# A streaming gradient: stores and loads on two queues in timed pairs, instead of one queue in triples

## The chip, the cores and the metric

The kernel runs on one core of a Trainium2 chip. A core has a vector engine (DVE), a scalar engine (ACT), GpSimd (POOL), a matrix engine that is not used here, and a sequencer for transfers (SP). SP, ACT and POOL can each issue DMAs; the bytes are moved by 16 DMA engines, from HBM to the on-chip memory SBUF (128 partitions) or back. The metric is device microseconds (us) for one execution; lower is better.

## What is computed

`reference(x)` is `np.gradient(x, axis=1)` for `x` of 8192 x 8192 float32. In each row, an inner element is half the difference of its right and left neighbours; the first element is `x[1] - x[0]`, the last `x[m-1] - x[m-2]`. Each element is read once and written once: 268.44 MB in, 268.44 MB out.

## The kernel before, in words

The 8192 rows are cut into 32 sets of 256 (`nsets`). A set puts two consecutive rows (`R = 2`) on each of 128 partitions, so that a partition holds 16,384 elements, 64 KiB, and one DMA moves 8.39 MB. There are three buffers, `slot0` to `slot2` (`NB = 3`); set i uses slot i mod 3. A slot is 64 elements (`SH`) wider than a set: the load writes at offset 64, the result is written from offset 0 in the same slot, so that the vector engine's pass writes behind where it reads.

For each set i, in the loop at lines 66 to 93:

- POOL (line 70) takes the four end differences of each partition's two rows into `ends`, as soon as the load has landed.
- DVE (line 76) makes one pass over 16,382 elements, a custom operation that subtracts two shifted views and halves, in place. It also writes wrong values at the row ends.
- The ends are copied over them (line 87), four elements per partition: by DVE for 20 sets, by POOL for 12.
- SP issues the store (line 89).
- After every third set SP issues the next three loads (lines 91 to 93, through `load`, line 60). Each of them waits until the store that last used the slot has landed.

Every DMA is issued by SP and goes into one queue, q1, in this order: loads 0, 1, 2, stores 0, 1, 2, loads 3, 4, 5, stores 3, 4, 5, and so on, to stores 30 and 31. The order within each engine is written out by hand (`manual_schedule`); `chain` (lines 45 to 56) tells the framework which steps an instruction must really wait for, and takes out the other dependences within a slot.

Of the kernel before, what the change touches and what calls it, by code (L numbers as in the profile page):

```python
# [1 line left out]

# [4 lines left out]


@with_exitstack
def kernel(  # L10
    ctx: ExitStack,
    tc: tile.TileContext,
    x: bass.AP,
    out: bass.AP,
):

    nc = tc.nc
    P = nc.NUM_PARTITIONS
    n, m = x.shape
    R = 2
    NB = 3  # L30
    SH = 64
    W = R * m
    nsets = n // (P * R)
    f32 = x.dtype

    x_sets = x.rearrange("(s p t) m -> s p (t m)", p=P, t=R)
    out_sets = out.rearrange("(s p t) m -> s p (t m)", p=P, t=R)

    pool = ctx.enter_context(tc.tile_pool(name="pool", bufs=1))
    slots = [pool.tile([P, SH + W], f32, name=f"slot{k}", tag=f"slot{k}") for k in range(NB)]  # L40
    ends = pool.tile([P, nsets, R, 2], f32, name="ends", tag="ends")
    loads, stores = [], [None] * nsets
    in_front = {}

    def chain(i, ins, *needed):

        group, engine = f"slot{i % NB}", ins.ins.engine
        keep = [o.ins for o in needed]  # L50
        if in_front.get(engine, (None,))[0] == group:
            keep.append(in_front[engine][1])
        tc.declare_no_dep(ins.ins, group=group, keep=keep, reason="implied by the needed step")
        tc.add_to_no_dep_group(group, ins.ins)
        in_front[engine] = group, ins.ins
        return ins

    def load(i):
        b = slots[i % NB]
        ins = nc.sync.dma_start(out=b[:, SH : SH + W], in_=x_sets[i])  # L60
        loads.append(chain(i, ins, *([stores[i - NB]] if i >= NB else [])))

    with tc.manual_schedule():
        for i in range(NB):
            load(i)
        for i in range(nsets):
            b = slots[i % NB]
            xin = b[:, SH : SH + W].rearrange("p (t m) -> p t m", m=m)

            ins = nc.gpsimd.tensor_sub(  # L70
                out=ends[:, i, :, :],
                in0=xin[:, :, 1 : m : m - 2],
                in1=xin[:, :, 0 : m - 1 : m - 2],
            )
            at = [chain(i, ins, loads[i])]
            ins = nc.vector._custom_dve(  # L76
                dve_ops.TENSOR_TENSOR_REDUCE_SUB_MAX,
                out=b[:, 1 : W - 1],
                in0=b[:, SH + 2 : SH + W],
                in1=b[:, SH : SH + W - 2],  # L80
                s0=0.0,
                s1=0.5,
            )
            halved = chain(i, ins, *at)
            res = b[:, 0:W].rearrange("p (t m) -> p t m", m=m)
            placer = nc.gpsimd if i % 5 in (1, 3) and i < nsets - 2 else nc.vector
            ins = placer.tensor_copy(out=res[:, :, 0 : m : m - 1], in_=ends[:, i, :, :])  # L87
            placed = chain(i, ins, halved)
            ins = nc.sync.dma_start(out=out_sets[i], in_=b[:, 0:W])
            stores[i] = chain(i, ins, placed)  # L90
            if i % NB == NB - 1:
                for k in range(i + 1, min(i + 1 + NB, nsets)):
                    load(k)


# [1 line left out]
_INS = ['x']  # L97
_OUTS = [((8192, 8192), 'float32')]


# [23 lines left out]
```

## Time and profile before

| what | value |
|---|---|
| time, median of 3 runs | 1247.73 us (1247.55 to 1247.99) |
| the profiled execution: span from first to last instruction | 1245.7 us |
| moved | 536.88 MB, 431 GB/s over the span |
| DVE pass over a set (line 76) | 32 of 17.224 us |
| DMA issue by SP | 0.34 us each at the median |
| DMA issue to landing, median | 58.0 us loads, 40.4 us stores (with the time in the queue) |

The profiled execution is one run of the program under the hardware profiler, with its own time; times inside it are compared with its span, not with the median of the runs. "Span" goes from the first instruction to the last. "Busy" is the time in which an engine executes instructions; issuing a DMA is not counted. The DMA row gives, in 40 equal slices of the span, the busy share of the 16 DMA engines in tenths (9 is 90% or more). A group's row reads: line, engine, operation, output<-input with shapes, count, then busy time, mean nanoseconds of one, and the idle time ahead of it with what ended it. A row of waits reads: who waited, for whom, us in total, times, longest. In the timeline a row is start, duration, engine, line, operation.

### The profile page before, as it was taken

The page shows a single profiled execution, that of the slowest core. Times are in us where ns is not written, and L with a number is a line of the kernel's source. Part 1 is how long each engine was busy: PE and PEld are TensorE (multiplying, and loading weights), DVE is VectorE, ACT ScalarE, POOL GpSimd, SP SyncE. Part 2 cuts the span into 40 slices and gives each one's busy share as a digit, 9 for nine tenths or more (in the row PEclk, how much of TensorE's full clock was granted, in tenths as well). Part 3 has the DMA queues.
Part 4 walks back from the last instruction along what each step waited for, and adds up shares of the span by engine and source line. Part 5 has one row for each costly group of instructions (what it writes and reads, how often), then busy time and mean ns, then how long its engine had stood idle before and what let it go on. Part 6 is the DMA issues. An engine that isn't in the chain of part 4 may idle for free.

```text
span 1245.7 us, 237 instructions
## 1 busy us (share of the span) xinstructions
DVE 554.6 (45%) x52; POOL 8.8 (1%) x48
## 2 busy tenths in 40 slices
DVE  2850583069009702850582079009603840591083
POOL 0000000000000000000000000000000000000000
DMA  9999999999999999999999999999999999999999
GB/s 404 438 436 423 427 431 438 438 438 436 436 427 431 425 438 436 425 434 436 429 434 436 434 436 434 436 434 438 419 436 436 434 438 438 431 434 429 429 410 404
DMA packets 9217, 536.88 MB, mean 431 GB/s; under 512 B 1024, under 2 KB 1024, under 8 KB 1024
## 3 DMA queue, kind: packets, MB, share of 16 engines
q1 hardware_dynamic: 9216, 536.88, 99.8%
q14 instruction: 1, 0.01, 0.0%
HBM read 268.44 MB, written 268.44 MB: 431 GB/s over the span
## 4 chain that ended last, share of the span: by engine, by line
another core or an unknown queue 74%; DVE 18%; DMA 3%; issue 2%; POOL 1%; SPq 0%; POOLq 0%
DVE slot L76 18%; DMA slot<-in_x_dram 3%; POOL ends L70 0%; POOL slot L87 0%; SPq L60 0%; POOLq L119 0%; DVE slot L87 0%
## 5 line engine op out<-in xcount | busy, mean ns | idle before, releaser
L76 DVE CUSTOM_DVE_ANT_0 slot<-slot 128x16382 f32<-128x16382 f32 x32 | 551.2, 17224 | 668.7 <-POOL ends L70 668.7
L70 POOL TENSOR_TENSOR ends<-slot 128x4 f32<-128x4 f32 x32 | 6.3, 198 | 989.6 <-DMA slot<-in_x_dram 989.6
L87 POOL COPY slot<-ends 128x4 f32<-128x4 f32 x12 | 2.3, 190 | 207.9 <-DVE slot L76 207.9
L87 DVE COPY slot<-ends 128x4 f32<-128x4 f32 x20 | 3.4, 172 | 0.7
L108 POOL MEMSET const-bfloat16-1.0<- 128x1 bf16 x1 | 0.1, 101 | 0.0
L108 POOL MEMSET const-uint8-127<- 128x1 uint8 x1 | 0.1, 101 | 0.0
L108 POOL MEMSET const-float32-0.0<- 128x1 f32 x1 | 0.1, 98 | 0.2 <-issue 0.2
L108 POOL MEMSET const-float32-1.0<- 128x1 f32 x1 | 0.1, 98 | 0.0
## 6 DMA issues: line engine op xcount, KB each, us to landing
slot<-in_x_dram SPq DMA_DIRECT2D x32, 58.0
out_dram<-slot SPq DMA_DIRECT2D x32, 40.4
```

What stands on the lines that cost most here:

```text
L70: ins = nc.gpsimd.tensor_sub(out=ends[:, i, :, :], in0=xin[:, :, 1 : m : m - 2], in1=xin[:, :, 0 : m - 1 : m - 2],)
L76: ins = nc.vector._custom_dve(dve_ops.TENSOR_TENSOR_REDUCE_SUB_MAX, out=b[:, 1 : W - 1], in0=b[:, SH + 2 : SH + W], in1=b[:, SH : SH + W - 2],
L87: ins = placer.tensor_copy(out=res[:, :, 0 : m : m - 1], in_=ends[:, i, :, :])
L108: nc = _bacc.Bacc("TRN2", target_bir_lowering=False, num_devices=1)
```

## The change

Loads stay on SP, stores go to ACT, which has its own queue. Two loads are issued at the start instead of three. From then on a store of set i and the load of set i + 2 (`ahead`) go as a pair:

- For sets 1 to 30, DVE first makes a pass over a tile of zeros (`still`), 2500 elements wide (`FIRST`), into the front part of the slot of set i + 2. It waits until store i - 1, the last user of that slot, has landed.
- Then DVE copies the ends of set i (for all sets; POOL copies none), and ACT issues store i.
- For sets 0 to 29, DVE makes a second pass over zeros, 1700 elements wide (`THEN`), into the same slot behind the first; SP issues load i + 2 when this pass is done.

The load overwrites what the two passes wrote, so the passes change nothing in the result. DVE's order for a set is: the pass over the set, the 2500-wide pass, the copy of the ends, the 1700-wide pass. POOL fills the zeros once at the start (128 x 2502).

```diff
-            placer = nc.gpsimd if i % 5 in (1, 3) and i < nsets - 2 else nc.vector
-            ins = placer.tensor_copy(out=res[:, :, 0 : m : m - 1], in_=ends[:, i, :, :])
+            ahead = i + NB - 1
+            if 0 < i < nsets - 1:
+                pause(ahead, SH, FIRST, stores[i - 1])
+            ins = nc.vector.tensor_copy(out=res[:, :, 0 : m : m - 1], in_=ends[:, i, :, :])
             placed = chain(i, ins, halved)
-            ins = nc.sync.dma_start(out=out_sets[i], in_=b[:, 0:W])
+            ins = nc.scalar.dma_start(out=out_sets[i], in_=b[:, 0:W])
             stores[i] = chain(i, ins, placed)
-            if i % NB == NB - 1:
-                for k in range(i + 1, min(i + 1 + NB, nsets)):
-                    load(k)
+            if ahead < nsets:
+                load(ahead, pause(ahead, SH + FIRST, THEN))
```

The start has `for i in range(NB - 1): load(i)`. New are

```python
    FIRST, THEN = 2500, 1700
    still = pool.tile([P, 2 + FIRST], f32, name="still", tag="still")
    nc.gpsimd.memset(still, 0.0)
    def pause(i, at, width, *needed):
        ins = difference(slots[i % NB][:, at : at + width], still, width)
        return chain(i, ins, *needed)
```

where `difference(out, x, width)` is the custom operation of line 76 with its shifted views, used for the set's own pass too. `load(i, *needed)` now waits for what it is given instead of the store of set i - 3.

More of the change, by code (lines that the diff above doesn't have):

```diff
@@ L56, in chain, with load, difference @@
         return ins
-    def load(i):
+    def load(i, *needed):
         b = slots[i % NB]
         ins = nc.sync.dma_start(out=b[:, SH : SH + W], in_=x_sets[i])
-        loads.append(chain(i, ins, *([stores[i - NB]] if i >= NB else [])))
+        loads.append(chain(i, ins, *needed))
+    def difference(out, x, width):
+        return nc.vector._custom_dve(
+            dve_ops.TENSOR_TENSOR_REDUCE_SUB_MAX,
+            out=out,
+            in0=x[:, 2 : 2 + width],
+            in1=x[:, 0:width],
+            s0=0.0,
+            s1=0.5,
+        )
+    def pause(i, at, width, *needed):
+        ins = difference(slots[i % NB][:, at : at + width], still, width)
+        return chain(i, ins, *needed)
     with tc.manual_schedule():
-        for i in range(NB):
+        for i in range(NB - 1):
             load(i)
@@ L75 @@
             at = [chain(i, ins, loads[i])]
[L76 to L83, printed above, removed]
+            ins = difference(b[:, 1 : W - 1], b[:, SH : SH + W], W - 2)
             halved = chain(i, ins, *at)
             res = b[:, 0:W].rearrange("p (t m) -> p t m", m=m)
-            placer = nc.gpsimd if i % 5 in (1, 3) and i < nsets - 2 else nc.vector
-            ins = placer.tensor_copy(out=res[:, :, 0 : m : m - 1], in_=ends[:, i, :, :])
+            ahead = i + NB - 1
+            if 0 < i < nsets - 1:
+                pause(ahead, SH, FIRST, stores[i - 1])
+            ins = nc.vector.tensor_copy(out=res[:, :, 0 : m : m - 1], in_=ends[:, i, :, :])
             placed = chain(i, ins, halved)
-            ins = nc.sync.dma_start(out=out_sets[i], in_=b[:, 0:W])
+            ins = nc.scalar.dma_start(out=out_sets[i], in_=b[:, 0:W])
             stores[i] = chain(i, ins, placed)
-            if i % NB == NB - 1:
-                for k in range(i + 1, min(i + 1 + NB, nsets)):
-                    load(k)
+            if ahead < nsets:
+                load(ahead, pause(ahead, SH + FIRST, THEN))
 _INS = ['x']
```

## The prediction

> **What bounds the kernel now.** I read the page's head with its DMA lines first, then the waits of SP's queue, the groups of instructions, the timeline of the end, and last the trace's packet records one by one (the rows behind the DMA lines). The page:
>
> ```profile
> span 1245.7 us, 237 instructions
> ...
> DVE 554.6 (45%) x52; POOL 8.8 (1%) x48
> ...
> DMA  9999999999999999999999999999999999999999
> ...
> q1 hardware_dynamic: 9216, 536.88, 99.8%
> ```
>
> One queue, q1, keeps the 16 DMA engines busy for 99.8% of the span; DVE has work for 45%. The end is set by how fast an engine passes its bytes and by holes between its packets. The packet records: 8192 packets of 65,536 bytes, 512 for each engine (8 for each load or store), and 1024 of 4 bytes, one behind every eighth. The big one takes 2.418 us at the median (5th percentile 2.418, 95th 2.422), which is 27.1 GB/s, and the next starts as one ends: a DMA takes an engine 8 x 2.418 = 19.34 us, a load and a store 38.69.
>
> So the span is: first packet at 1.75, its extra latency 0.62 (3.04 against 2.42), 512 x 2.418 = 1238.0, then 4.1 of other losses, and 1.18 from the last packet's end (1244.49) to the end (1245.67). Of the 4.1 some 3.2 stand in one place: the last packet of a third load, ahead of the first store of a triple. At these ten switches from load to store the slowdown is 0.01 to 1.11 us per engine, mean 0.32. Switches from store to load show 0.02, load to load and store to store nothing.
>
> With holes and switches free, the span would be 1.75 + 0.62 + 1238.0 + 1.18 = **1241.6**: 4.1 us, 0.33%, is all that reordering can win while packets take 2.418 each.
>
> What sets the order today:
>
> ```profile
> SPq L89 <- DVE slot L87: 525.6, 20, 55.9
> SPq L60 <- DMA out_dram<-slot: 373.1, 29, 19.3
> SPq L89 <- POOL slot L87: 300.1, 12, 36.9
> ```
>
> SP waits for nearly the whole span, with packets of earlier DMAs still queued below. Nothing waits long enough to leave the engines empty, except at the end:
>
> ```profile
> 1204.42 0.17 DVE L87 COPY slot<-ends 128x4 f32<-128x4 f32 x1
> 1204.62 19.69 SPq L89 DMA_DIRECT2D out_dram<-slot  x2
> ```
>
> Set 30's store, issued at 1204.62, met engines that had just run dry: its first packets start at 1205.47 to 1205.59, so issue to first packet is 0.85 to 0.97 us. Those packets took 2.45, only 0.03 over the rest.
>
> **The change, part by part.** Profiled span against profiled span; the median of the runs (1247.73) stands 2.06 above the span and I add that at the end.
>
> *Passes on DVE.* From
>
> ```profile
> L76 DVE CUSTOM_DVE_ANT_0 slot<-slot 128x16382 f32<-128x16382 f32 x32 | 551.2, 17224 | 668.7 <-POOL ends L70 668.7
> ...
> L87 DVE COPY slot<-ends 128x4 f32<-128x4 f32 x20 | 3.4, 172 | 0.7
> ```
>
> a pass of 2500 costs 2500/16382 x 17.224 = 2.63 us by proportion, or 2.77 if the 0.172 of a 4-element copy is a fixed part; 1700 costs 1.79 or 1.94. I take 2.70 and 1.87. Thirty of each (sets 1 to 30, sets 0 to 29) add 137 us, and 12 copies move from POOL to DVE (12 x 0.17 = 2). DVE then has 694 us of work, 22.0 per set against 38.7 of DMA: no bound. The memset of the zeros on POOL, up to 3 us by DVE's pace, stands before set 0's subtraction, which waits for a landing at 22.64; it is hidden.
>
> *Wait for a landing ahead of the store.* Behind DVE's wait stand this set's 4-element copy, its store, the second pass, and the load two sets on. So store i goes only after store i-1 has landed, and the load goes one pass behind it; of each kind one is in flight. Today's slack of two queued DMAs is gone. From the end of store i-1's last packet to the first packet of store i: landing 0.36 (81.39 to 81.76; 1244.49 to 1244.84), to DVE 0.05 (SP took 0.02, POOL 0.08), pass 2.70, copy with its start 0.21, to the issue 0.03, to the first packet 0.91. Together **4.3 us**; the ends are 4.1 and, with the 1.70 that the slowest engine's very first packet took from issue, 5.1.
>
> *What covers these 4.3 us* is what is left of the load then. It arrives 1.87 + 0.03 = 1.9 us behind its store. If the engine takes turns packet by packet and the load's first packet is second in line, store and load alternate and one load packet, 2.42, is left: 1.9 us of idling, in 30 pairs 56 us. If the second store packet is already chosen by then, two are left, 4.84: no hole. If it finishes a whole DMA before it turns to the other queue, 19.3 are left: no hole. No row shows two queues, so the cost per pair lies between 0 and 1.9. Nearest is the first load packet's 0.62 us of latency, which later ones do not show: an engine begins the next packet at least that much before the last ends. That is enough for a load that comes 1.9 us into a packet of 2.42, and two packets are left; but then the next store waits 0.5 us for the last of them, its load comes only 1.4 us into a packet, and 0.62 no longer does. As 0.62 is a lower bound and two of the three orders give no hole, I take 0; the middle one has a margin of 0.5 us.
>
> The Trainium skill, "DMA: Bandwidth & Descriptors", section "Queues, rings and completion order", has each engine going round its queues and draining a whole packet of typically 9 to 17 descriptors before it switches. A DMA here leaves 9 records per engine, so by that rule it might be one such unit and the hole 0; the trace lists the eight pieces as packets of their own, by which it would be 1.9.
>
> *Switches.* Today there are 10 from load to store. The new order has at least 31, and up to 8 per pair, some 250, if packets alternate. By today's mean the first is 31 x 0.32 = 9.9 us, 5.8 more than all of today's 4.1; the second is 80 us. Below nothing: if one queue's read ran beside the other's write, each could win; but no packet at today's 20 switches took under 2.415, so I allow 5 us of gain at most. I take 0, since the slow packet stands where both transfers share one queue in order, and bounds of -5 and +80.
>
> *Start and end.* Load 2 goes behind store 0 instead of ahead of it; load 1's packets run to 41.6 and store 0 is issued at 40.4, so its packets are there at 41.3. The end stays: store 30 covers set 31's 17.2 us of DVE with 19.3 us of transfer. Cost 0; without the cover it would be a few us, once.
>
> **Sum.** 1245.7 - 4.1 + 0 + 0 = 1241.6 of span; with 2.06 on top **1243.6**, 0.33% faster.
>
> **Rivals.**
> 1. *One load packet is left* (slower). Place: the end of every pair. Price: 4.3 - 2.42 = 1.9 us, x 30 = 56, so 1243.6 + 56 = 1299; if it hits every second pair, as a look ahead of just 0.62 us would have it, 28 us, 1271. It decides from the point where the load's packet is taken second. For it: taking turns is the plain order for two queues, and the gap of 4.3 us is the surest number here. Against: the orders with two or eight packets left.
> 2. *Every handover pays the load-to-store switch*: 31 x 0.32, span 1241.6 + 9.9 = 1251.5, time 1253.5. For it: ten of ten switches show something. Against: 0.01 at the weakest.
> 3. *Every alternation pays it*: 80 us, 1323, with rival 1 up to 1380.
> 4. *Nothing changes*: the holes and switches of the new order cost about what today's 4.1 do, 1245 to 1250. In the same page of the Trainium skill, section "Issuing engines are not separate DMA queues", DMAs of SP and ACT end on the same 16 engines and a second issuer saves issue time alone; the trace agrees in that SP issues in 0.34 us a DMA of 19.3.
> 5. *Packets of two queues overlap* and pass faster than 2.418: below 1238. Against: 27.1 GB/s on each engine, flat over 7299 of 8192 packets to within 1 ns.
>
> **How the numbers follow.** The forecast has 0.38, rival 5 0.04, so faster 0.42. Rival 4 has 0.11. Rival 1 has 0.22, rival 2 0.12, rival 3 0.13, so slower 0.47. Two tenths of a per cent, 2.5 us, is about what a measurement of this kernel can tell from no change. Both signs are open: the forecast's own range is 1238 to 1245.2. The range from 1236 to 1302 takes in the forecast, rivals 1, 2 and 4 and part of rival 5; rival 3 and the rest, some 0.15, stay outside.
>
> **What would show it.** Right: DMA share still 99% or more in all 40 slices, two queues with 50% each, big packets at 2.42 in the mean, DVE waiting for a landing in front of each 2500-wide pass. Rival 1: DMA share near 95%, 1.9 us without packets at each pair's end. Rivals 2 and 3: share at 99%, but packets ahead of store packets longer than 2.42. Rival 5: packets of both queues open at once and over 440 GB/s. Wrong altogether if DVE or an issue, not a landing, turns out last in front of the stores.

## The result, and the profile after

The changed kernel takes 1334.81 us (median of 4 runs, 1334.1 to 1336.45) against 1247.64 for the kernel before (4 runs): a ratio of 1.0699, interval 1.0684 to 1.0714. It is 7% slower, outside the forecast's range. The page of the profiled execution:

```profile
span 1333.2 us, 325 instructions
...
DVE 691.5 (52%) x124; POOL 29.0 (2%) x37
...
DMA  9999999999999999999999999999999999999999
GB/s 409 409 378 423 395 409 409 378 433 385 409 409 378 423 395 409 409 378 409 409 407 397 391 409 409 409 407 380 409 409 409 407 380 409 409 409 409 378 425 393
...
q1 hardware_dynamic: 4608, 268.44, 49.3%
q10 hardware_dynamic: 4608, 268.44, 48.4%
```

The busy tenths still show 9 in all 40 slices, so that row alone would say that nothing happened. The row of GB/s and the shares say more: two queues with half of the bytes each, 97.7% together, and slices of 378 to 433 GB/s. So there are holes of about 2%, and they are less than a third of the loss. The rest is inside the busy share: packets that take longer.

The packet records (the rows behind the DMA lines: start, duration, size, queue) give the split. They do not name the engine, so I chained them: a packet belongs to the engine on which one has just ended. Across a hole several engines fit, and the chain there is a choice. A big packet beyond its usual 2.418 us counts as *long* by what it exceeds. Per engine, long packets sum to 4.2 us before and 64.3 after. Of the 87.5 us by which the span grew, 60.1 are long packets; the other **27.4** are holes. This split is used for all runs below.

The big packets of one such chain over a pair, start and duration in us, S for stores (queue q10), L for loads (q1), from the records:

```
S406.44(2.42) L408.86(2.42) L411.28(2.42) L413.69(2.42)        <- end of a pair: last S, three L left
S417.33(2.47) S419.80(2.44) S422.23(3.45) L425.68(2.97)        <- next pair: 1.2 us without a packet, then long ones
S428.64(2.42) L431.06(2.42) S433.47(2.42) L435.89(2.42) ...    <- then in turn, 2.418 each, for the rest of the pair
```

Three things are to be seen. Store and load packets take turns one by one, and this costs next to nothing (2047 loads in the middle of L, S, L, S exceed 2.418 by 0.04 us in the mean, 2524 stores in the middle of S, L, S, L by 0.00). The load, issued 1.8 us behind its store, comes in only after two or three store packets. And the long packets sit there: third S and first L, together about 2 us in every pair.

The holes and the long packets do not go together. Every second pair begins with all 16 engines dry (without a packet), for 1.5 to 2.0 us in the mean, as this one does; the pairs between begin with 4 to 10 engines dry, 0.03 to 0.25 us in the mean over all 16. Yet the long packets of pairs 2 to 30 sum to 1.9 to 2.1 us in the first kind and 2.0 to 2.5 us in the second.

The timeline at the same handover:

```profile
413.61 2.76 DVE L56 CUSTOM_DVE_ANT_0 slot<-still 128x2500 f32<-128x2500 f32 x1 [20.49 <-DMA out_dram<-slot]
416.29 0.17 DVE L88 COPY slot<-ends 128x4 f32<-128x4 f32 x1
416.36 1.92 DVE L56 CUSTOM_DVE_ANT_0 slot<-still 128x1700 f32<-128x1700 f32 x1
416.49 0.34 ACTq L90 DMA_DIRECT2D out_dram<-slot  x1
```

DVE's 2500-wide pass starts at 413.61, when the store before has landed. But the last packet of that store ended at 410.86 on the slowest engine: the landing takes 2.75 us here, where I had counted 0.36. A DMA leaves a 4-byte record behind its eighth packet, and with another queue waiting that record takes its turn too, one load packet (2.42) later. From the pass on, the sum was right: 2.76, 0.17 with its start, 0.03, and 0.84 to the first packet at 417.33. So the way is 6.5 to 6.8 us instead of 4.3, and what covers it is two load packets (4.84) on most engines here, three (7.25) on the others.

And the waits:

```profile
POOL ends L76 <- DMA slot<-in_x_dram: 1263.5, 32, 42.8
DVE slot L56 <- DMA out_dram<-slot: 586.4, 30, 20.8
```

DVE waits 586 us in all for landings ahead of its 2500-wide passes, so DVE's 692 us of work bound nothing; the landing is last there, as forecast.

### The profile page after: what moved, and what is told of

The parts are those of the page before. It is cut to its first block, busy times and chain, and to the rows that moved or that the text cites. A ratio compares the mean times of both kernels' runs of the same rounds, so it can differ in the third digit from the quotient of the medians.

```text
span 1333.2 us, 325 instructions
## 1 busy us (share of the span) xinstructions
DVE 691.5 (52%) x124; POOL 29.0 (2%) x37
## 2 busy tenths in 40 slices
DMA packets 9217, 536.88 MB, mean 403 GB/s; under 512 B 1024, under 2 KB 1024, under 8 KB 1024
## 4 chain that ended last, share of the span: by engine, by line
DMA 86%; DVE 9%; issue 3%; POOL 0%; POOLq 0%
DMA out_dram<-slot 81%; DVE slot L56 9%; DMA slot<-in_x_dram 5%; DVE slot L88 0%; POOL ends L76 0%; POOLq L119 0%
## 5 line engine op out<-in xcount | busy, mean ns | idle before, releaser
L56 DVE CUSTOM_DVE_ANT_0 slot<-still 128x1700 f32<-128x1700 f32 (+1 forms) x60 | 140.2, 2343 | 586.4 <-DMA out_dram<-slot 586.4
L76 POOL TENSOR_TENSOR ends<-slot 128x4 f32<-128x4 f32 x32 | 26.7, 833 | 1263.5 <-DMA slot<-in_x_dram 1263.5
```

The costliest lines, as they stand in the source:

```text
L56: return nc.vector._custom_dve(dve_ops.TENSOR_TENSOR_REDUCE_SUB_MAX, out=out, in0=x[:, 2 : 2 + width], in1=x[:, 0:width], s0=0.0, s1=0.5,)
L76: ins = nc.gpsimd.tensor_sub(out=ends[:, i, :, :], in0=xin[:, :, 1 : m : m - 2], in1=xin[:, :, 0 : m - 1 : m - 2],)
```

## The experiments

Holes were explained by these records. What makes packets long was not, and the experiments were made for that. All are edits of the changed kernel except the fifth. The first theory was that a queue that had run empty and starts beside the running one pays ("late start"). It fell; the second is that engines that run dry get into step, and that a change of direction in step is what costs. It explains a part. Results together, each ratio against runs of the kernel before made with it (medians 1247.5 to 1248.5), the split against the one span of before (1245.7):

| run | time us | ratio to before, interval | span | long packets | holes and rest |
|---|---|---|---|---|---|
| changed kernel | 1334.81 | 1.0699, 1.0684 to 1.0714 | 1333.2 | +60.1 | +27.4 |
| one queue | 1249.76 | 1.0016, 1.0007 to 1.0026 | 1247.7 | +0.4 | +1.6 |
| both passes 4 wide | 1382.39 | 1.1077, 1.1058 to 1.1095 | 1381.8 | +64.5 | +71.6 |
| second pass 4 wide | 1460.81 | 1.1707, 1.1690 to 1.1725 | 1458.1 | +64.5 | +147.9 |
| first pass 4 wide | 1302.21 | 1.0434, 1.0418 to 1.0449 | 1299.1 | +47.8 | +5.6 |
| two queues, no pairs | 1258.31 | 1.0108, 1.0043 to 1.0174 | 1247.9 | -1.6 | +3.8 |
| load ahead of store | 1455.96 | 1.1668, 1.1644 to 1.1691 | 1455.3 | +46.5 | +163.1 |
| shifted source | 1334.87 | 1.0697, 1.0676 to 1.0719 | 1333.4 | +61.3 | +26.4 |
| two load queues | 1335.71 | 1.0704, 1.0683 to 1.0725 | 1335.1 | +17.3 | +72.1 |
| second pass 3400 | 1297.63 | 1.0396, 1.0380 to 1.0411 | 1296.9 | +36.5 | +14.7 |
| first 2500, second 2 x 2500 | 1299.47 | 1.0403, 1.0386 to 1.0420 | 1298.9 | +49.0 | +4.2 |
| one queue, run dry | 1493.42 | 1.1964, 1.1940 to 1.1988 | 1491.6 | +24.5 | +221.4 |
| never dry | 1253.04 | 1.0044, 1.0027 to 1.0061 | 1251.6 | +1.5 | +4.4 |

### One queue

```diff
-            ins = nc.scalar.dma_start(out=out_sets[i], in_=b[:, 0:W])
+            ins = nc.sync.dma_start(out=out_sets[i], in_=b[:, 0:W])
```

> Stores go back to SP's queue, with pairs, waits and both passes as in the changed kernel. Theory (the time goes into what two queues do at a handover: the load joins a running store 2 us late per pair, the store's last 4-byte record waits a turn, and then the engines run dry): with one queue there is no turn and no joining, a store's landing leaves 19 us of load to cover 4.3 us, so no hole; 31 switches from load to store at 0.32 us: 1247 to 1255 us. Rival A (the passes and the wait for a landing are on the path by themselves): 1330 us or more. Rival B (what costs is that HBM goes from loads to stores and back 31 times with the engines in step, 1.1 us as at the first switch of before): 1278 us.

Measured: 1249.76 us, as the theory had it. All passes, waits and pairs are still there:

```profile
span 1247.7 us, 325 instructions
...
DVE 691.7 (55%) x124; POOL 8.8 (1%) x37
...
q1 hardware_dynamic: 9216, 536.88, 99.6%
```

The same 124 DVE instructions with the same work, the same landings to wait for, and 85 us less. The passes over zeros are not on the path; a store's landing now takes 0.36 to 0.45 us in all 30 pairs, and the load behind it covers the rest. The single changes of direction tell more. The first four, in order, cost 0.07, 0.96, 1.13 and 0.00 us per engine, the next ones 0.38, 0.01, 0.28, and from then on at most 0.2, while the spread of the 16 engines behind the change (the time from the first engine's first packet to the last engine's) grew from 0.5 to 1.9, 2.8, 3.6 and at last 5.2 us. In the kernel before, the first change to a store costs 1.10 us (spread 0.6). This is what led to the second theory. The rest of the kernel before does not fit it well: the change back to loads at that same spread costs 0.02, the next one to stores 0.19, and of the later ones the dearest are 0.42 and 0.63, at spreads of 1.2 to 2.0.

### The passes, one by one

Short diffs: `FIRST, THEN = 4, 4`, then `2500, 4`, then `4, 1700`.

> Both passes 4 elements wide instead of 2500 and 1700; the waits and the two queues stay. Theory: a store is at the engines 2.4 + 1.7 = 4.1 us after the last packet of the store before, while two or three packets of the load (4.8 to 7.3 us) are left, so no hole (28.7 us gone), and the next load comes before its queue has run empty, so the joining (some 57 us) goes too: 1245 to 1262 us. Rival A (each us of pass is a us of time): the passes cost 140 us, so it would be near 1200, below what the packets allow. Rival B (every change of direction at a handover costs, whether a queue was empty or not): 1300 to 1310, only the hole gone.

> First pass 2500 as before, second pass 4 elements wide: load 0.2 us behind its store. Theory: the load is taken one or two packets earlier, one or two of its packets are left when the store ends, and the hole grows by up to a packet: 1.9 to 4.3 us a pair; the joining stays: 1340 to 1400 us. Rival (the 1700-wide pass is a cost of its own): 1.9 x 30 = 56 us less, 1278 us.

> First pass 4 elements wide, second pass 1700 as before. Theory: as with both passes short the store comes 4.1 us after the one before ended, three load packets (7.3 us) are left, no hole; the load comes while its queue still holds packets, no joining: 1243 to 1262 us. Rival (joining costs by the 1.9 us between store and load, whatever is in the queue): 1300 to 1310 us.

Measured: 1382.39, 1460.81 and 1302.21 us, all three above the theory's ranges; the third is in its rival's. The second was slower than the changed kernel and the third faster, as forecast; the first went the wrong way. Where store and load go at once (the first two kernels), the load is second in line and packets alternate from the start, S, L, S, L, to the end: one load packet (2.42) is left, and the way is 3.9 us and 6.5: 1.5 and 4.1 us of hole on the slowest engine, more on those ahead of it. Measured are 71.6 / 30 = 2.4 us a pair and 147.9 / 30 = 4.9. So rival 1 of the prediction, one packet left, is real, and the 1700-wide pass is what the changed kernel avoids it with: taking that pass out costs 126 us (1460.81 against 1334.81). The first pass costs 33 us (1334.81 against 1302.21), two thirds of it holes. Long packets stay, 64.5, 64.5 and 47.8 us against 60.1: they are a cost of their own. The theory of the late start had expected them to go with the short passes.

### Two queues without pairs

The kernel before with the edit of its store line alone, `nc.sync` to `nc.scalar`.

> The kernel before with one edit: stores are issued by ACT, so they have a queue of their own; triples, no passes over zeros, no wait of a store for the store before. Theory (a queue that ran empty and starts beside the other running one costs 1.5 to 2.2 us each time; steady alternation of packets costs nothing): no holes, two to three such starts per triple, 10 triples: 1265 to 1310 us. Rival A (two queues cost nothing by themselves, only pairs that wait for a landing do): 1245 to 1250 us. Rival B (each change of direction between packets costs): over 1320 us.

Measured: 1258.31 us, the median of four runs of 1249.81, 1250.8, 1265.82 and 1267.57; the profiled one is the first. Two lie at rival A's range and two in the theory's. What sets the two groups apart was not followed, and the slower one has no profile. In the profiled run long packets sum to 2.6 us, less than before.

```profile
DMA  9999999999999999999999999999999999999997
...
q1 hardware_dynamic: 4608, 268.44, 49.8%
q10 hardware_dynamic: 4608, 268.44, 49.6%
```

Packets of two queues take turns for 1248 us, queues run empty and start again beside the other some 30 times, and nothing is lost in this run. That speaks against the theory of the late start, and against any theory in which two queues or alternating directions cost 60 us by themselves; the never-dry kernel below, whose four runs agree, ends both. The one long stretch is the first meeting (1.0 us), while the engines are still in step from the start. None of them runs dry afterwards until the end. At 85.5 us a load joins running stores while the engines are spread by no more than 0.65 us, and the pair pays only 0.14.

### Order, address, direction

Load ahead of the store (4-wide pass and load first, then the 1700-wide pass, copy and store); `in_=source(i)` with x read 1024 elements further on; and

```diff
-            ins = nc.scalar.dma_start(out=out_sets[i], in_=b[:, 0:W])
+            if i < nsets - 2:
+                ins = nc.scalar.dma_start(out=b[:, 0:W], in_=x_sets[i])
+            else:
+                ins = nc.scalar.dma_start(out=out_sets[i], in_=b[:, 0:W])
```

> Order in a pair turned round: after the landing and the 2500-wide pass a 4-wide pass and the load go first, then the 1700-wide pass (over the zeros themselves), the copy and the store. The load ends first, so nothing covers the way from a store's landing to the next pair: 4.3 us of hole in 30 pairs, 130 us. Theory (the late starter pays, whichever it is): another 1.5 to 2.2 us a pair, now at the store's first packet and the load packet ahead of it: 1420 to 1440 us. Rival (only a load that starts beside a running store pays, since HBM must turn from writes to reads): no long packets, 1370 to 1380 us.

> The changed kernel, but loads read x 4 KB further on (for all sets but the last; the output is then of shifted data), so that load and store addresses no longer agree in their low bits. Theory (late start of a queue): no change, 1331 to 1339 us. Rival (load and store packets that start in step meet in the same HBM channels): the long packets go, some 55 us less, 1275 to 1285 us.

> The changed kernel, but ACT's transfer is a load as well (set i once more into its slot, in place of the store; only the last two sets are stored). Both queues now move HBM to SBUF. Theory (late start of a queue, whatever it moves): long packets as before, 1320 to 1340 us. Rival (the long packets come from reads that start among writes): none of them, only the hole of 0.9 us a pair, 1265 to 1275 us.

Measured: 1455.96, 1334.87 and 1335.71 us. The first is above both of its ranges, since the holes are 163 us and not 130. With the load first, its first two packets are long, by 0.7 and 1.0 us. The 0.7 is what the first load packet takes longer on idle engines, as the third kernel shows; the 1.0, with a store arriving, is the price of mixing, paid whichever comes first. A shift by 4 KB changes nothing; that one shift is all that was tried on addresses. With two load queues the time is the theory's but the split is not: long packets fall to a third, and those left are the first packet of each pair alone (0.65 us, what a first load packet from an idle engine takes longer). No packet is long where the second queue joins. The holes grow to 72 us since two packets are left there, not three, in every pair. So it takes both directions to make packets long beyond that first one.

### Running dry

`FIRST, THEN = 4, 3400`; then 2500 with the second pass made twice; then the one-queue kernel with nine passes of 2500 behind the landing.

> First pass 4 elements, second pass 3400 wide (3.6 us) instead of 1700: a store comes 4.1 us after the one before ended, and three to four load packets (7.3 to 9.7 us) are left, so that no engine runs dry. Theory (running dry brings the 16 engines into step, and changing direction in step costs about 2 us a pair; engines that never run dry drift apart and then pay nothing): losses in the first pairs only, 1245 to 1258 us. Rival (a store and a load that start within a few us of each other cost 1 to 2 us a pair, in step or not): 1275 to 1305 us.

> First pass 2500 as in the changed kernel, second one 2 x 2500 wide (5.5 us): the store comes 6.7 us after the one before ended, four or more load packets (9.7 us) are left. Theory (dry engines get into step): no engine runs dry, 1245 to 1258 us although 100 us of passes are added on DVE. Rival (starts near each other cost): 1275 to 1305 us. Rival (passes on the path): over 1400 us.

> One queue (stores on SP), and nine passes of 2500 in place of the first one, so that the store behind a landing comes about 25 us after the store before ended, when the 19.3 us of load behind that one are over: all engines run dry in every pair, some 5 to 6 us, 150 to 180 us in all: 1400 to 1430 us. What tells theories apart are the long packets beyond the first of each store: theory (in step, each change of direction costs) 0.7 to 1.2 us at the change from store to load in every pair, 20 to 36 us per engine in all; rival (only two queues cost): under 6 us per engine, as in the one-queue kernel that never runs dry (4.6).

Measured: 1297.63, 1299.47 and 1493.42 us. The first two missed the theory's range and fell into the rival's, 1275 to 1305: I had counted on three to five load packets being left and engines never dry, but a store that waits for a packet has its load closer behind, and the second 4-byte turn was in the way. With 3400, pairs alternate strictly. A pair that begins with about 1 us of hole pays 2.0 to 2.2 us in long packets, the next, with none, 0.4 to 0.7. With 2 x 2500 some engines run dry in about half of the pairs, by 0.1 to 0.9 us in the mean, and nearly all pairs pay 1.0 to 2.1, even those in which I find no hole. The kernel with the first pass 4 wide does the same: its pairs without a hole pay 0.9 to 2.1. That is not explained by dryness.

The one-queue kernel gave the clean case. Its time missed the 1400 to 1430 us expected, since the holes are 7.4 us each and not 5 to 6; its long packets came out as the theory had them. Of one period, the load-and-store stretch and the hole:

```profile
605.00:624.70 19.70, 18.52 (x2) 0.00 (x0) 1.00 1.02 426
624.70:644.50 19.80, 17.94 (x7) 0.00 (x0) 1.00 0.98 424
644.50:652.00 7.50, 7.43 (x5) 0.21 (x1) 1.00 0.00 0
```

(Columns: stretch, its length, DVE busy, POOL busy, clock, DMA share, GB/s.) The store fills the first stretch, the load the second, and then no byte moves for 7.4 us. All engines start the next store within 0.15 us of each other, and each change from store to load 19 us later costs 0.77 to 0.94 us, in period after period; the one-queue kernel that does not run dry pays this at its first change from store to load and then nothing there. One queue, one direction at a time, no late start: having run dry 20 us before is enough. Whether it acts through the step is argued, not shown, since here the two come together.

### Never dry, and two that were spoiled

```diff
-    FIRST, THEN = 2500, 1700
+    FIRST, THEN = 4, 3400
...
+                pause(ahead, SH + FIRST, THEN)
+                pause(ahead, SH + FIRST, THEN)
                 load(ahead, pause(ahead, SH + FIRST, THEN))
```

> First pass 4 elements, and three passes of 3400 (11 us) between store and load: half of the load is left when the store ends, against a way of 4.1 us to the next store, so that no engine can run dry. Theory (running dry puts the engines in step, a change of direction in step costs): the first pairs pay, the engines drift apart as in the one-queue kernel, and then nothing is paid: long packets under 12 us per engine in all, 1245 to 1258 us. Rival (in pairs each start of a load beside a young store costs, dry or not): 1.5 us a pair, 45 us of long packets, 1290 to 1300 us.

> The one-queue kernel that runs dry in every pair, with a load of 47 KB into each of 8 partitions put ahead of the stores of sets 1 to 29 in the same queue (data that the set's load overwrites later): it occupies 8 of the 16 engines for 1.7 us, so that the two halves start the store 1.7 us apart. Theory (in step): the long packets at the change from store to load, 28.7 us per engine, fall to under 15. Rival (having been dry costs, in step or not): 26 to 32 us.

> The changed kernel with the same load of 47 KB on 8 partitions ahead of the stores of sets 1 to 29, on ACT's queue; the set's load now also waits for it, and comes some 3.7 us behind the store instead of 1.9. Theory (in step): long packets, 64 us per engine, fall to under 40; the time falls with them, less about 0.9 us a pair for the added bytes: 1290 to 1315 us. Rival (late start or having been dry costs): 58 to 66 us of long packets, 1330 us or more.

Measured: 1253.04 us for the first, as the theory had it.

```profile
span 1251.6 us, 385 instructions
...
DVE 888.6 (71%) x184; POOL 14.2 (1%) x37
...
q1 hardware_dynamic: 4608, 268.44, 49.8%
q10 hardware_dynamic: 4608, 268.44, 49.6%
```

DVE has 197 us more work than in the changed kernel, two queues still mix in pairs behind a landing of 2.75 us, and the time is 82 us lower. Four or five load packets are nearly always left at the end of a store (9.7 to 12.1 us), the way is 3.9 (as with both passes short). The first pair pays 1.9 us, pairs 2 to 30 pay 0.0 to 0.4, but for one with 0.8. Each queue starts beside the other after mostly 5 to 7 us without packets of its own, so a late start as such is cheap.

This edit changes two things: no engine runs dry, and the load comes 11 us behind its store instead of 1.8. So a rival stands: a load that starts soon behind a store costs. The packet records help to sort. Here are pairs 2 to 30 of the changed kernel and of six others (both, second and first pass 4 wide, shifted source, second pass 3400, 2 x 2500), whose load comes 0.1 to 5.5 us behind its store:

| spread of the engines at the store's first packet, us | engines that ran dry ahead of it | pairs | long packets, us a pair |
|---|---|---|---|
| under 0.3 | 12 to 16 | 87 | 1.9 to 2.3 |
| 0.3 to 1.0 | 12 to 16 | 21 | 1.8 to 2.2 |
| 0.3 to 1.6 | 2 to 11 | 57 | 1.5 to 2.5 |
| 0.3 to 1.6 | 0 or 1 | 22 | 0.9 to 2.1 |
| 2.0 to 2.5 | 0 or 1 | 16 | 0.4 to 0.7 |

So the spread sorts these pairs better than the hole does: dry engines start close together, but engines close together pay without a hole too. It is a sorting after the fact, not a test, and it has exceptions. Seven pairs of the never-dry kernel start at a spread of 1.1 to 1.2 us and pay nothing; there the load is far behind the store.

The two staggered kernels took 1658.33 and 1550.67 us, since the inserted transfer, 47 KB on each of 8 partitions, took 5.6 us per engine at the median instead of 1.7 and slowed the store packets beside it; the sums of long packets (40.2 and 85.1) mean nothing for the question. One detail of the first still does: at the change from store to load, far behind the inserted transfer, only 8 packets were long per period instead of 21, and the cost was 0.41 to 0.44 us per engine instead of 0.77 to 0.94. The half of the engines that came first paid, the other half, 4 to 5 us later, did not. That fits the theory of the step; as a test it is weak.

## Why the prediction was wrong

- **Read of what bounds the kernel: right.** 2.418 us per packet, 1238.0 in all, at most 4.1 us to gain. No run here went under it, and no packet of two queues overlapped.
- **Passes on DVE: right.** 2.76 and 1.92 us against 2.70 and 1.87; hidden, as one queue shows.
- **The way from one store to the next: failed in its first term.** "Landing 0.36" holds for one queue. With two, the 4-byte record waits a turn: 2.75. The rest of the sum came out within 0.2 us.
- **What covers it: the middle order was right, the margin was not.** Two or three packets are left, 4.84 or 7.25, against 6.5 to 6.8. The forecast's 0 became 27.4 / 30 = 0.9 us a pair, as 1.5 to 2.0 in every second pair and little in the others. The 27.4 us are close to the 28 that rival 1 has for every second pair, but that is luck in the number: two packets were left against 6.5 us, not one against 4.3. The rule quoted from the Trainium skill, "DMA: Bandwidth & Descriptors", section "Queues, rings and completion order", that a whole packet of 9 to 17 descriptors is drained before the switch, would have given no hole; here each 64 KiB piece, and each 4-byte record, takes its own turn, so the measurement decides.
- **Switches: this is the step that failed most.** "I take 0, since the slow packet stands where both transfers share one queue in order." The cost is neither per handover (rival 2: one queue makes 31 at 0.4 us more than before) nor per alternation (rival 3: two queues without pairs make hundreds for nothing), though the time landed near rival 3's number. It is paid once a pair, where both directions first mix while the engines run close together: 2 us a pair, 60.1 us in all, against a term of 0. The reason given for the 0 fails as well, since the slow packets came with two queues. There was a mark of it in the trace of before: 1.10 us at the first change to a store, 0.01 to 0.63 at the others. I took the mean of ten and did not ask why they differ.
- **Rival 4:** the rule of the Trainium skill quoted there, that a second issuer saves issue time alone, agrees with two queues without pairs and never dry, neither of which was faster than before, and is silent on the 7% that pairs cost.

What was shown: the holes; that passes and waits by themselves cost nothing; that both directions are needed; that the long packets go where no engine is dry and the load follows late (never dry, 1.5 us more than before), and that with one queue, running dry brings them back (24.5). What is argued: that what counts is how close together the 16 engines run. What stays open: why a change of direction then costs 1 to 2 us, why some changes at a small spread cost nothing, and how much the late load of the never-dry kernel does by itself. No version beat the kernel before; the one-queue pairs come nearest, 0.16% behind.

## What to carry to other kernels

A DMA row full of 9s hides both a 2% hole and packets that have grown by 5%: read GB/s by slice, then the packets. When two queues share the engines, a landing comes a turn of the other queue later, so a chain "landing, compute, next issue" needs more cover than on one queue. Keep transfers queued so that engines never run dry, and let a second direction join late: the pairs here cost 0.9 us of hole each in the mean, and 2 us of long packets.

## What the runs showed of the hardware that was not expected

- A queue that gets work while the other runs is served only after one to three more packets of the other (2.4 to 7.3 us), so 1.7 us of delay at issue moved its start by a packet or two, worth 126 us in all.
- POOL's 4-element subtraction takes 198 ns, but 1552 ns where it starts during DVE's 1700-wide pass (at 416.79, the pass ran from 416.36 to 418.28); it ended with the pass. Off the path here.

```profile
416.79 1.55 POOL L76 TENSOR_TENSOR ends<-slot 128x4 f32<-128x4 f32 x1 [40.93 <-DMA slot<-in_x_dram]
```

- A load of 47,104 bytes on each of partitions 0 to 7 kept 8 engines busy for 5.6 us each, a third of the 27.1 GB/s that each gives on 128 partitions.
